# Mask rooms, mask loads and pinned copies in a single-core step of a hybrid decoder

## The chip, the cores and the metric

The kernel runs on one core of one Trainium2 chip. A core has a matrix engine (PE, with PEld for its weight loads), three elementwise engines (DVE, ACT, POOL) and SP, which only starts DMAs; ACT and POOL can start DMAs too. Each engine works through its own list of instructions in order and waits where an instruction needs something that another engine or a DMA hasn't finished. The metric is device time in microseconds (us) of one execution, and the median of some executions is compared. About 1%, some 9 us here, is what a measurement of this kernel can tell from no change.

## The reference, cut to what matters

One layer of a decoder for 1024 new prompt tokens and 8 single sampled tokens. All float32.

```python
proj = rms_norm(x, norm_g) @ w_in          # b, c, u, z (convolution), q, kv (3 branches), gates, z (attention)
q = rope(rms_norm(q, q_gain), pos) * HEAD_DIM ** -0.5
k = rope(rms_norm(kv[..., 0, :, :], k_gain), pos)
conv = b * (short_conv(c * u) + bias) * silu(z_conv)
kv_cmp = einsum('bcrjgd,rjde->bcjge', blocks_of_32(kv[cmp]) + cmp_pe, cmp_w)
# attention of a query block of 128: three branches, each with a mask of its own
for br in (cmp, slc, win):
    p = masked_softmax(q @ k_br.T, mask_br)
    o += sigmoid(gate[br]) * (p @ v_br)
y = x + concat([conv, o * silu(z_attn)]) @ w_out
sample_win_kv = concat([state_win_kv, new_row])[:, 1:]     # 8 state windows, moved by one row
```

## The kernel before, in words

Precision is kept by splitting each matrix operand in a high part (ACT's copy, `wh`, `hH`) and a low part (the difference, `wl`, `hL`, by DVE or POOL, line L80 for all of them), so each product is three matmuls.

**Stage 1** (`phase0`, 0 to 224 us) normalizes and transposes the tokens and projects them, tile by tile: first the rows of the compressed branch (`kv_tile` with branch 0), then those of the selected branch, then `gps`, the compression of 32-row blocks (64 matmuls of 66 columns, line L702), then the window branch, then the queries. Merged into it run the channel-wise products of one weight (`chan_mm`, lines L223 to L225, results in `mixA`). `norm_rope` (L262 to L273) is the chain of ACT and DVE operations that normalizes and rotates a tile's rows. `token_pairs` (L425) writes finished rows of the compressed branch into a tile `pr` by four DMAs, and `cmp_transposes` (L433) transposes `pr` on PE, so the PE's list holds a place at which it needs those DMAs. `cw_fetch` (L447) loads the compression weights in four chunks, each by four DMAs into the one room that has the tag `wx`, and each is split by ACT and DVE (tile `cw`) before `gps` can use it. `small_things` (L472 to L496) transposes a few small tables on PE: its `per2` is a copy by POOL (L476) into a room named `qn`, which `norm_rope` uses too.

**Attention** (`attn_stream`, 224 to about 660 us) goes over 32 units (a query block of 128, a group, a head pair). `prep` transposes the query (L903) and splits it (`q1`, `q2`); then scores (L931), softmax (DVE L919 with the mask tile, ACT L921), scaling (POOL L976, L980), transposes of P (L1005), their split, and the products with v (L1015). `masks` allocates the mask tile, clears part of it (POOL L881) and loads the rest by four DMAs (L883). Between the units stand the convolution's channel products (again L223 to L225, each followed by ACT L808 and DVE L809, which read the result out of its bank so that a later product may use it). `gate_rows` (16 small DMAs into `gr` and `grh`) and `window_copy` (8 copies of 511 KB from DRAM to DRAM, L864) are written among units 6 to 21; nothing reads them before the sample part late in the kernel.

The order on each engine isn't that of the code: a list scheduler places instructions by its own costs, and it may put one that is written late far ahead. `tc.keep_in_program_order`, which the change calls `keep`, holds an instruction behind all that was traced before it on its engine; it adds no wait. Rooms in SBUF are given by pools, and a tile that takes a room over waits for the last user of it.

Of the kernel before, what the change touches and what calls it, by code (L numbers as in the profile page):

```python
# [10 lines left out]
F32 = mybir.dt.float32  # L11
# [3 lines left out]
OP = mybir.AluOpType  # L15
# [5 lines left out]
NT = 9  # L21
# [40 lines left out]
def hymba_step_kernel(ctx, tc, io):  # L62
    nc = tc.nc
    WARM = 8
    PE, ACT, DVE, POOL, SP = nc.tensor, nc.scalar, nc.vector, nc.gpsimd, nc.sync
    SB, PSUM = bass.MemoryType.SB, bass.MemoryType.PSUM

# [3 lines left out]
    def f(ap):  # L71
        return ap.bitcast(F32)
# [38 lines left out]
    gr = cst.tile([64, 3], F32, name="gr")  # L111
    grh = cst.tile([32, 2, 3], F32, name="grh")
# [26 lines left out]
    for c in range(3):  # L139
        n = min(CH, NTOK - c * CH)  # L140
# [93 lines left out]
    rope0 = g2 = None  # L234

    def rope_tables(gain, slot, scale):

        SP.dma_start(g2[:, 0], bcast_rows(gain, 64))
        h0 = bass.AP(tensor=gain.tensor, offset=gain.offset + 32, ap=[[0, 128], [1, 32]])
        SP.dma_start(g2[:, 1, 0:32], h0)  # L240
        SP.dma_start(g2[:, 1, 32:64], bcast_rows(gain, 32))
        if scale != 1.0:
            DVE.tensor_scalar(g2, g2, scale, None, op0=OP.mult)
        v = mCf[:, 1152 + 1152 * slot:2304 + 1152 * slot].rearrange("p (i t d) -> p i t d", i=2, t=NT)
        for i in range(2):
            POOL.tensor_tensor(v[:, i], rope0[:, i], g2[:, i][:, None, :].to_broadcast([128, NT, 64]), OP.mult)
        return v[:, 0], v[:, 1]

    E0 = (ACT, POOL)
# [98 lines left out]
    wp = ExitStack()  # L348
    wk = wp.enter_context(pool("w0", "right"))
    rope0 = mCf[:, 0:1152].rearrange("p (i t d) -> p i t d", i=2, t=NT)  # L350
    hS = wk.tile([128, 8, 40], F32R, name="hS")
    POOL.memset(f(hS), 0.0)
    g2 = wk.tile([128, 2, 64], F32, name="g2", bufs=2)
    junk = mCf[:, 3456:3968].bitcast(mybir.dt.bfloat16)
    ROWS, ENDS = 2, 14000
    wl0 = w_loader(wk, 280, 2, 2, 1, 9)
    g1 = mCf[0:1, 2304:3328]
    one = mCf[0:1, 3968:4096]
# [8 lines left out]
    xsp = xss.enter_context(pool("xs"))  # L367
# [104 lines left out]
    def small_things():  # L472

        cvr, per, pti, spread = (small_in[n] for n in ("cvr", "per", "pti", "spread"))
        per2 = wk.tile([128, 512], F32, name="qn")[:32, :256].rearrange("p (j r d) -> p j r d", j=2, r=2)
        POOL.tensor_copy(per2, per.rearrange("p (j d) -> p j d", j=2)[:, :, None, :].to_broadcast([32, 2, 2, 64]))  # L476
        ptf = wk.tile([8, 16], F32, name="ptf")
        copy(DVE, ptf, pti)
        p = bank("tp")
# [11 lines left out]
        for r in range(2):  # L491
            q = slice(r * 64, r * 64 + 64)
            v = pv[q, :, :, r][:, :, None, :].to_broadcast([64, 2, 2, 16])
# [361 lines left out]
    def gate_rows(b):  # L855

        g = gates[b:b + 1, 8, :].rearrange("o (r t) -> o r t", t=3)
        SP.dma_start(gr[b * 8:(b + 1) * 8], g)
        SP.dma_start(grh[b % 4 * 8:b % 4 * 8 + 8, b // 4], g)

    def window_copy(b):

        src, dst = state_win[b], s_win[b]
        SP.dma_start(bass.AP(tensor=dst.tensor, offset=dst.offset, ap=[[8176, 16], [1, 8176]]),  # L864
                     bass.AP(tensor=src.tensor, offset=src.offset + 256, ap=[[8176, 16], [1, 8176]]))

    mask = P0 = wmask = None

    def masks():
        nonlocal mask, P0, wmask  # L870

        for v in (gates[:, 0:8], gates[:8, 8]):
            ACT.activation(v, v, AF.Tanh, scale=0.5)
            DVE.tensor_scalar(v, v, 1.0, 0.25, op0=OP.add, op1=OP.mult)
        POOL.memset(cu[:, 0:2], 0.0)


        mask = at.tile([128, 1212], F32, name="mask")
        P0 = at.tile([128, 2, 128], F32, name="P0")
        wmask = bass.AP(tensor=mask.tensor, offset=mask.offset, ap=[mask.ap[0], [832, 2], [1, 320]])  # L880
        POOL.memset(mask[:, 128:1024], 0.0)  # L881
        for dst, src, n in ((0, 0, 128), (1024, 512, 128), (1152, 864, 32), (1184, 644, 28)):
            SP.dma_start(mask[:, dst:dst + n], io["c_mask"][:, src:src + n])  # L883
        POOL.memset(P0, 0.0)


# [2 lines left out]
    def attn_stream():  # L889
        units = [(qi, g, hp) for qi in range(8) for g in range(2) for hp in range(2)]  # L890

        def double(u):
            qi, g, hp = u
            c = qi % 2 * 256 + hp * 128
            qd = at.tile([128, 2, 2, 64], F32, name="qd")
            v = qp[qi // 2][g][:, c:c + 128].rearrange("p (i d) -> p i d", i=2)
            POOL.tensor_copy(qd, v[:, :, None, :].to_broadcast([128, 2, 2, 64]))
            return qd

        def prep(qd):  # L900
            p = bank("pt")
            for i in range(2):
                PE.transpose(p[:, i * 128:i * 128 + 128], qd[:, i].rearrange("p r d -> p (r d)"), ident)  # L903
            q1 = at.tile([128, 2, 128], F32R, name="q1", bufs=2)
            q2 = at.tile([128, 2, 128], F32R, name="q2", bufs=2)
            pv = p[:, :256].rearrange("p (i c) -> p i c", i=2)
            copy(ACT, q1, pv)
            sub(DVE, q2, pv, f(q1))
            return q1, q2
# [111 lines left out]
        def finish(u, o):  # L1021
# [9 lines left out]
            if g == 1 and hp == 1:  # L1031
                done[qi] = True

        qq = prep(double(units[0]))
        masks()
        pend = []
        for ui, u in enumerate(units):
            o = [None]
# [715 lines left out]
```

## Time and profile before

| | |
|---|---|
| median of three runs | 928.27 us (921.03, 928.27, 930.33) |
| profiled execution | 926.67 us, its span 924.8 us |
| PE busy | 873.1 us (94%) |
| mean granted clock of PE | 0.983 |
| DVE, ACT, POOL busy | 577.0, 533.7, 402.3 us |
| DMA bytes | 91.12 MB, 99 GB/s over the span |

PE is the engine that the kernel waits for nearly all the time. A busy PE can still be slow: the profile gives the granted clock in shares of the higher of two levels (1.00 is 2.4 GHz, 0.50 is 1.2 GHz), and at 0.50 the same matmuls take twice as long while the busy share stays full. So lost time is read in two places, idle time of PE and stretches with a clock under 1.00.

### The profile page before, as it was taken

The numbers are of one execution on the slowest core, as the hardware profiler recorded it, in microseconds if no ns is written. First come the engines' busy times: TensorE is split into PE (matmuls) and PEld (weight loads), VectorE is DVE, ScalarE is ACT, GpSimd is POOL, SyncE is SP. The second block draws the span as 40 slices with busy tenths as digits, with TensorE's granted clock in tenths as the row PEclk, the third lists the DMA queues.
The fourth block names the chain that finished last, engine by engine and source line by source line (L and its number), as shares of the span: only waits on it lengthen the run. The fifth ranks groups of instructions, "written<-read, shape, count | busy, mean of one in ns | idle before, by whom it ended". The sixth has DMA issues, their size and how long they took to land.

```text
span 924.8 us, 16581 instructions
## 1 busy us (share of the span) xinstructions
PE 873.1 (94%) x5769; PEld 781.2 (84%) x5769; DVE 577.0 (62%) x1482; ACT 533.7 (58%) x1350; POOL 402.3 (44%) x547
## 2 busy tenths in 40 slices
PE   8889899999899999999989999999989999999987
PEld 6889899998689898899979898999877788677765
DVE  5866636687455555865775667667746555765663
ACT  5543325444466565665565755665756766687761
POOL 4332311112345444454344444444655444677751
PEclk9999979999889999999999999999999999999999
DMA  7433331651101000100010000000878552667621
GB/s 260 124 88 91 94 115 58 210 178 44 34 8 40 23 24 24 24 23 9 16 35 24 24 6 19 24 1 1 256 258 285 205 196 92 236 211 245 220 68 47
DMA packets 67154, 91.12 MB, mean 99 GB/s; under 512 B 19192, under 2 KB 49344, under 8 KB 64895
## 3 DMA queue, kind: packets, MB, share of 16 engines
q1 hardware_dynamic: 59004, 52.32, 18.7%
q0 software_dynamic: 8064, 37.75, 12.3%
q8 instruction: 45, 0.74, 0.4%
q14 instruction: 39, 0.31, 0.1%
q10 hardware_dynamic: 2, 0.00, 0.0%
HBM read 77.92 MB, written 15.29 MB: 101 GB/s over the span
## 4 chain that ended last, share of the span: by engine, by line
PE 47%; ACT 7%; DVE 7%; POOL 3%; issue 3%; DMA 2%; SPq 0%; ACTq 0%; DVEq 0%; POOLq 0%
PE o L1015 7%; PE pt L1005 5%; PE s L931 5%; PE mm L225 5%; PE mm L224 5%; PE mm L223 5%; POOL P L980 2%; PE om L1160 2%; PE mm L1572 1%; PE mm L1573 1%; PE mm L1574 1%; PE o L1456 1%; ACT P L921 1%; PE pt L1139 1%; PE s L1328 1%
## 5 line engine op out<-in xcount | busy, mean ns | idle before, releaser
L223 PE MATMUL mm<-hH,wh 128*128 128x384 f32 (+1 forms) x480 | 157.9, 329 | 3.7 <-DVE mixC L809 2.1
L225 PE MATMUL mm<-hH,wl 128*128 128x384 f32 (+1 forms) x480 | 155.0, 323 | 0.4 <-POOL wl L80 0.2
L224 PE MATMUL mm<-hL,wh 128*128 128x384 f32 (+1 forms) x480 | 154.8, 322 | 0.0
L80 POOL TENSOR_TENSOR wl<-wraw,wh 128x256 fp32r<-128x256 f32 (+1 forms) x105 | 77.6, 755 | 156.4 <-ACT wh L76 143.6
L921 ACT ACTIVATE P<-P,stat 128x640 f32<-128x640 f32 (+7 forms) x192 | 113.1, 591 | 36.8 <-DVE stat L919 36.1
L80 DVE TENSOR_TENSOR pl<-pt,ph 128x512 fp32r<-128x512 f32 (+1 forms) x164 | 102.7, 635 | 50.2 <-ACT ph L76 48.9
L76 ACT ACTIVATE ph<-pt 128x512 fp32r<-128x512 f32 (+1 forms) x164 | 88.4, 548 | 71.9 <-PE pt L1005 70.7
L980 POOL TENSOR_SCALAR P<-P,stat,gates 128x640 f32<-128x640 f32 (+7 forms) x128 | 99.9, 789 | 57.7 <-DVE stat L971 46.1
L1005 PE MATMUL pt<-ident,P 128*128 128x128 f32 x592 | 96.9, 281 | 6.2 <-POOL P L980 3.3
L931 PE MATMUL s<-k,q 128*128 128x320 f32 (+8 forms) x416 | 97.5, 337 | 2.5 <-DVE q L80 1.5
L223 PEld LDWEIGHTS mm<-hH,wh 128*128 128x128 f32 x480 | 91.1, 190 | 5.5 <-DVE mixC L809 3.3
L210 PE MATMUL mm<-wh,hL 128*128 128x256 f32 (+1 forms) x320 | 92.8, 291 | 1.6 <-DVE hL L80 1.6
L208 PE MATMUL mm<-wh,hH 128*128 128x256 f32 (+1 forms) x320 | 93.9, 294 | 0.1
L209 PE MATMUL mm<-wl,hH 128*128 128x256 f32 (+1 forms) x320 | 92.7, 290 | 0.9 <-POOL wl L80 0.9
L225 PEld LDWEIGHTS mm<-hH,wl 128*128 128x128 f32 x480 | 91.3, 190 | 1.1 <-POOL wl L80 1.0
L224 PEld LDWEIGHTS mm<-hL,wh 128*128 128x128 f32 x480 | 91.4, 190 | 0.2
L919 DVE CUSTOM_DVE_ANT_0 P<-s,mask 128x32 f32<-128x32 f32 (+8 forms) x160 | 70.9, 472 | 29.5 <-PE s L931 25.1
L1005 PEld LDWEIGHTS pt<-ident,P 128*128 128x128 f32 x592 | 71.0, 141 | 20.6 <-POOL P L980 10.6
L1015 PE MATMUL o<-ph,v 128*128 128x256 f32 x264 | 75.0, 303 | 1.7 <-ACT ph L76 1.1
L1015 PE MATMUL o<-pl,v 128*128 128x256 f32 x264 | 74.3, 303 | 1.6 <-DVE pl L80 1.5
L931 PEld LDWEIGHTS s<-k,q 128*128 128x128 f32 x416 | 67.9, 193 | 6.7 <-DVE q L80 1.7
L210 PEld LDWEIGHTS mm<-wh,hL 128*128 128x128 f32 x320 | 62.4, 195 | 2.0 <-DVE hL L80 2.0
(385 smaller groups left out, 2058.1 us busy)
## 6 DMA issues: line engine op xcount, KB each, us to landing
wraw<-in_w_in_dram SPq DMA_DIRECT2D x54, 256.0 KB
wo<-wo_d POOLq DMA_DIRECT2D x8, 512.0 KB, 4.6
out_s_win_dram<-in_state_win_kv_dram SPq DMA_DIRECT2D x8, 511.0 KB
xr<-in_x_prompt_dram SPq DMA_DIRECT2D x14, 256.0 KB
out_y_prompt_dram<-xr SPq DMA_DIRECT2D x14, 256.0 KB
sd<-in_state_win_kv_dram SPq DMA_DIRECT2D x5, 512.0 KB
mixA<-in_x_prompt_dram SPq DMA_DIRECT2D x4, 512.0 KB
xt<-in_x_prompt_dram SPq DMA_DIRECT2D x4, 512.0 KB
```

The costliest lines, as they stand in the source:

```text
L80: return eng.tensor_tensor(out, a, b, OP.subtract)
L208: PE.matmul(o[:, :n], hH[t // 3][:, k, s], wh, start=k == 0, stop=False)
L209: PE.matmul(o[:, :n], hH[t // 3][:, k, s], wl, start=False, stop=False)
L210: PE.matmul(o[:, :n], hL[t // 3][:, k, s], wh, start=False, stop=k == 7)
L223: PE.matmul(o[:, :n], wh, hH[c][:, k], start=k == 0, stop=False)
L224: PE.matmul(o[:, :n], wh, hL[c][:, k], start=False, stop=False)
L225: PE.matmul(o[:, :n], wl, hH[c][:, k], start=False, stop=k == 7)
L921: return lambda: ACT.activation(P, P, AF.Exp, bias=stt[:, 0, c:c + 1], scale=-1.0, accum_out=stt[:, 1, c:c + 1])
L931: PE.matmul(s[:, a:b], q[:, i], k, start=first, stop=not first)
L980: POOL.tensor_scalar(P[:, i, :n], P[:, i, :n], stt[:, 2, c + i:c + i + 1], gates[:, qi, gt:gt + 1], op0=OP.mult, op1=OP.mult)
L1005: PE.transpose(p[:, y * 256 + i * 128:y * 256 + i * 128 + 128], src[:, i], ident)
L1015: PE.matmul(o[0][:, :256], v, X[:, y * 256:y * 256 + 256], start=br == 1 and x == 0 and y == 0 and X is h[0], stop=last and y + 1 == len(p ...
```

## The change

It does five things. The rooms `rows` and `wx` are allocated ahead of all others of their pool, which moves the addresses: attention's mask tile now lies over `rows` and no longer over rooms that the last query's `norm_rope` uses. The four mask loads are issued by ACT, and `masks` is written ahead of the first `prep`, with the gates' sigmoids split out and left behind it. `per2` gets a tile of its own. `gate_rows` and `window_copy` are pinned on SP, and the two operations that build q's rotation table are pinned on POOL.

```diff
--- before.py
+++ after.py
@@ -62,6 +62,8 @@
 def hymba_step_kernel(ctx, tc, io):
     nc = tc.nc
     WARM = 8
+
+    keep = tc.keep_in_program_order
     PE, ACT, DVE, POOL, SP = nc.tensor, nc.scalar, nc.vector, nc.gpsimd, nc.sync
     SB, PSUM = bass.MemoryType.SB, bass.MemoryType.PSUM
 
@@ -243,7 +245,9 @@
             DVE.tensor_scalar(g2, g2, scale, None, op0=OP.mult)
         v = mCf[:, 1152 + 1152 * slot:2304 + 1152 * slot].rearrange("p (i t d) -> p i t d", i=2, t=NT)
         for i in range(2):
-            POOL.tensor_tensor(v[:, i], rope0[:, i], g2[:, i][:, None, :].to_broadcast([128, NT, 64]), OP.mult)
+            r = POOL.tensor_tensor(v[:, i], rope0[:, i], g2[:, i][:, None, :].to_broadcast([128, NT, 64]), OP.mult)
+            if scale != 1.0:
+                keep(r)
         return v[:, 0], v[:, 1]
 
     E0 = (ACT, POOL)
@@ -348,11 +352,14 @@
     wp = ExitStack()
     wk = wp.enter_context(pool("w0", "right"))
     rope0 = mCf[:, 0:1152].rearrange("p (i t d) -> p i t d", i=2, t=NT)
+    ROWS, ENDS = 2, 14000
+
+    wk.tile([128, 512], F32, name="rows", bufs=ROWS)
+    wk.tile([128, 2, 280], F32, name="wx")
     hS = wk.tile([128, 8, 40], F32R, name="hS")
     POOL.memset(f(hS), 0.0)
-    g2 = wk.tile([128, 2, 64], F32, name="g2", bufs=2)
+    g2 = wk.tile([128, 2, 64], F32, name="g2")
     junk = mCf[:, 3456:3968].bitcast(mybir.dt.bfloat16)
-    ROWS, ENDS = 2, 14000
     wl0 = w_loader(wk, 280, 2, 2, 1, 9)
     g1 = mCf[0:1, 2304:3328]
     one = mCf[0:1, 3968:4096]
@@ -472,7 +479,7 @@
     def small_things():
 
         cvr, per, pti, spread = (small_in[n] for n in ("cvr", "per", "pti", "spread"))
-        per2 = wk.tile([128, 512], F32, name="qn")[:32, :256].rearrange("p (j r d) -> p j r d", j=2, r=2)
+        per2 = xsp.tile([32, 256], F32, name="per2").rearrange("p (j r d) -> p j r d", j=2, r=2)
         POOL.tensor_copy(per2, per.rearrange("p (j d) -> p j d", j=2)[:, :, None, :].to_broadcast([32, 2, 2, 64]))
         ptf = wk.tile([8, 16], F32, name="ptf")
         copy(DVE, ptf, pti)
@@ -855,24 +862,26 @@
     def gate_rows(b):
 
         g = gates[b:b + 1, 8, :].rearrange("o (r t) -> o r t", t=3)
-        SP.dma_start(gr[b * 8:(b + 1) * 8], g)
-        SP.dma_start(grh[b % 4 * 8:b % 4 * 8 + 8, b // 4], g)
+        keep(SP.dma_start(gr[b * 8:(b + 1) * 8], g))
+        keep(SP.dma_start(grh[b % 4 * 8:b % 4 * 8 + 8, b // 4], g))
 
     def window_copy(b):
 
         src, dst = state_win[b], s_win[b]
-        SP.dma_start(bass.AP(tensor=dst.tensor, offset=dst.offset, ap=[[8176, 16], [1, 8176]]),
-                     bass.AP(tensor=src.tensor, offset=src.offset + 256, ap=[[8176, 16], [1, 8176]]))
+        keep(SP.dma_start(bass.AP(tensor=dst.tensor, offset=dst.offset, ap=[[8176, 16], [1, 8176]]),
+                          bass.AP(tensor=src.tensor, offset=src.offset + 256, ap=[[8176, 16], [1, 8176]])))
 
     mask = P0 = wmask = None
 
-    def masks():
-        nonlocal mask, P0, wmask
+    def sigmoids():
 
         for v in (gates[:, 0:8], gates[:8, 8]):
             ACT.activation(v, v, AF.Tanh, scale=0.5)
             DVE.tensor_scalar(v, v, 1.0, 0.25, op0=OP.add, op1=OP.mult)
         POOL.memset(cu[:, 0:2], 0.0)
+
+    def masks():
+        nonlocal mask, P0, wmask
 
 
         mask = at.tile([128, 1212], F32, name="mask")
@@ -880,7 +889,7 @@
         wmask = bass.AP(tensor=mask.tensor, offset=mask.offset, ap=[mask.ap[0], [832, 2], [1, 320]])
         POOL.memset(mask[:, 128:1024], 0.0)
         for dst, src, n in ((0, 0, 128), (1024, 512, 128), (1152, 864, 32), (1184, 644, 28)):
-            SP.dma_start(mask[:, dst:dst + n], io["c_mask"][:, src:src + n])
+            ACT.dma_start(mask[:, dst:dst + n], io["c_mask"][:, src:src + n])
         POOL.memset(P0, 0.0)
 
 
@@ -1031,8 +1040,9 @@
             if g == 1 and hp == 1:
                 done[qi] = True
 
+        masks()
         qq = prep(double(units[0]))
-        masks()
+        sigmoids()
         pend = []
         for ui, u in enumerate(units):
             o = [None]
```

What it moves: first PE, in stage 1. Tile `tp_850` (`tp_852` after) is the bank of `small_things`, `mm_905` the last product of the compressed branch, `mm_970` a channel product. Before:

```order
L212 MATMUL mm_905<-wh_206,hS_120 40x256
L484 MATMUL tp_850<-ident_58,qn_846 128x32 x2
L213 MATMUL mm_905<-wl_207,hS_120 40x256
L212 MATMUL mm_905<-wh_210,hS_120 40x256
L213 MATMUL mm_905<-wl_211,hS_120 40x256
L223 MATMUL mm_970<-hH0_96,wh_635 128x384
```

After, the two transposes of `per2` stand with the other small ones:

```order
L440 MATMUL tp_820<-ident_58,pr1_224 128x128 x4
L488 MATMUL tp_852<-ident_58,cvr_221 128x20 x4
L489 MATMUL tp_852<-ident_58,ptf_850 16x8
L491 MATMUL tp_852<-ident_58,per2_848 128x32 x2
L226 MATMUL mm_873<-hL2_101,wh_236 128x264
```

And seven matmuls into `mm_1010`, the first tile of the selected branch, PE now needs the last `pr` tile (`pr1_224`):

```order
L211 MATMUL mm_1010<-wl_480,hH0_96 128x256
L212 MATMUL mm_1010<-wh_479,hL0_97 128x256
L210 MATMUL mm_1010<-wh_545,hH0_96 128x256
L440 MATMUL tp_933<-ident_58,pr1_224 128x128 x4
L507 MATMUL tp_940<-ptT_860,spread_222 128x8
L510 MATMUL tp_940<-ptT_860,spread_222 128x4 x2
L211 MATMUL mm_1010<-wl_546,hH0_96 128x256
```

Before, the same four transposes stood 57 matmuls further on, in the next tile's product: the wait on `qn` is gone from the list, and the need for `pr` is earlier.

Second DVE, ahead of `gps`: the split of the fourth chunk of compression weights (`cw`). Before it stood behind the sample rows of the selected branch:

```order
L266 TENSOR_TENSOR qn<-srows_90,rs 8x128
L267 TENSOR_TENSOR srows_90<-qn,mixC 8x128
L271 TENSOR_TENSOR rb<-qn,mixC 8x2x32 x2
L273 TENSOR_TENSOR srows_90<-srows_90,rb 8x128
L80 TENSOR_TENSOR cw<-cwr,cw 128x8x64
L80 TENSOR_TENSOR wl<-wx,wh 128x280
```

After, it stands inside the rows of the third pair of tiles:

```order
L270 TENSOR_TENSOR qn<-rows,rs 128x256
L271 TENSOR_TENSOR rows<-qn,mixC 128x256
L275 TENSOR_TENSOR rb<-qn,mixC 128x4x32 x2
L82 TENSOR_TENSOR cw<-cwr,cw 128x8x64
L277 TENSOR_TENSOR rows<-rows,rb 128x256
L82 TENSOR_TENSOR k_1004<-tp,k_1004 64x2x256
L79 COPY kd_1279<-rows 128x512
L82 TENSOR_TENSOR wl<-wraw,wh 128x280 x2
```

It moved ahead of all the sample rows and the weight splits, and on PE the 64 matmuls of `gps` now stand in one piece, where before 20 matmuls of the window branch stood between the first 24 and the other 40.

Third DVE, where attention begins. `mm_2986`, `mm_3075` and `mm_3167` are the three parts of a channel product (128, 128 and 8 columns of tokens); L919 is the masked part of the softmax. Before:

```order
L80 TENSOR_TENSOR q2_2954<-pt_2950,q1_2953 128x256
L809 SCALAR_TENSOR_TENSOR mixC_75<-mixC_75,mm_2986 128x384
L809 SCALAR_TENSOR_TENSOR mixA_76<-acc_3207,mixA_76 128x4x128
L80 TENSOR_TENSOR q2_3038<-pt_3034,q1_3037 128x256
L809 SCALAR_TENSOR_TENSOR mixA_76<-acc_3315,mixA_76 128x4x8
L809 SCALAR_TENSOR_TENSOR mixA_76<-acc_3696,mixA_76 128x4x128
L809 SCALAR_TENSOR_TENSOR mixA_76<-acc_4302,mixA_76 128x4x128
L809 SCALAR_TENSOR_TENSOR mixC_75<-mixC_75,mm_3075 128x384
L809 SCALAR_TENSOR_TENSOR mixC_75<-mixC_75,mm_3167 128x264
L919 ISA P1_2970,stat_2972<-s_2975,mask_2962 128x128
L919 ISA stat_2972 128x1
```

After:

```order
L82 TENSOR_TENSOR q2_2964<-pt_2960,q1_2963 128x256
L928 ISA P1_2972,stat_2974<-s_2977,mask_2950 128x128
L928 ISA stat_2974 128x1
L928 ISA P1_2972,stat_2974<-s_3015,mask_2950 128x128
L928 ISA stat_2974 128x1
L928 ISA P0_2951,stat_2974<-s_2977,mask_2950 128x32
L928 ISA stat_2974 128x1
L928 ISA P0_2951,stat_2974<-s_3015,mask_2950 128x32
L928 ISA stat_2974 128x1
L816 SCALAR_TENSOR_TENSOR mixA_76<-acc_3028,mixA_76 128x4x128
L928 ISA P2_2973,stat_2974<-s_3031,mask_2950 128x128
L928 ISA stat_2974 128x1
```

The softmax of the first unit now stands right behind its query's split, ahead of the read-out of the channel products, which before came first. On PE the second and third part of that product, before in one piece, are now cut by the first units' transposes and products.

## Rows read from the trace of the kernel before

**Rows 1.** What PE waited for, 0 to 240 us: total us, times, longest.

```profile
PE tp L484 <- POOL qn L476: 2.7, 1, 2.7
...
PE gps L702 <- DVE cw L80: 2.6, 1, 2.6
```

**Rows 2.** Stretches: length, busy us of PE, PEld, DVE, ACT, POOL, PEclk, DMA, GB/s.

```profile
60.00:72.00 12.00, 9.33 (x68) 8.97 (x67) 6.67 (x19) 5.15 (x15) 8.61 (x12) 1.00 0.24 60
116.00:128.00 12.00, 12.00 (x62) 11.90 (x61) 3.29 (x9) 3.59 (x13) 2.61 (x3) 0.57 0.70 218
228.00:262.00 34.00, 28.50 (x134) 23.43 (x132) 17.26 (x71) 16.96 (x60) 12.87 (x28) 0.80 0.13 35
```

**Rows 3.** Shorter stretches of the beginning of attention, same columns.

```profile
234.00:236.00 2.00, 2.00 (x7) 2.00 (x7) 1.30 (x2) 0.63 (x1) 0.00 (x0) 0.50 0.00 0
...
250.00:252.00 2.00, 2.00 (x11) 2.00 (x11) 1.21 (x9) 1.07 (x5) 0.00 (x0) 0.50 0.51 127
```

**Rows 4.** Timelines where attention begins: start, length, engine, line, operation, count, [idle <- releaser].

```profile
231.72 0.45 PE L931 MATMUL s<-k,q 128*128 128x160 f32 x2 [1.46 <-DVE q L80]
...
259.38 1.52 PE L1005 MATMUL pt<-ident,P 128*128 128x128 f32 x4
...
231.26 0.41 DVE L80 TENSOR_TENSOR q<-pt,q 128x256 fp32r<-128x256 f32 x1
...
243.34 0.28 DVE L919 CUSTOM_DVE_ANT_0 P<-s,mask 128x128 f32<-128x128 f32 x1
...
225.74 1.28 ACT L808 ACT_TABLE_LOAD   x1
...
228.06 1.77 SPq L883 DMA_DIRECT2D mask<-in_c_mask_dram  x4
```

**Rows 5.** Timeline of PE around the two transposes of `per2`.

```profile
63.47 0.28 PE L212 MATMUL mm<-wh,hS 128*40 128x256 f32 x1
66.42 0.31 PE L484 MATMUL tp<-ident,qn 32*128 32x32 f32 x2 [2.67 <-POOL qn L476]
...
67.04 0.34 PE L223 MATMUL mm<-hH,wh 128*128 128x384 f32 x1
...
71.21 0.28 PE L208 MATMUL mm<-wh,hH 128*128 128x256 f32 x1
```

**Rows 6.** Timelines of POOL and of DVE around the copy and `norm_rope`.

```profile
60.51 4.47 POOL L80 TENSOR_TENSOR wl<-wraw,wh 128x256 fp32r<-128x256 f32 x6 [15.00 <-ACT wh L76]
65.73 0.64 POOL L476 COPY qn<-mixC 32x256 f32<-32x256 f32 x1 [0.75 <-DVE rb L271]
...
62.02 0.70 DVE L196 SCALAR_TENSOR_TENSOR rs<-rs 128x4 f32<-128x4 f32 x1
...
65.69 0.43 DVE L273 TENSOR_TENSOR rows<-rows,rb 128x256 f32<-128x256 f32 x1
...
67.30 0.22 DVE L80 TENSOR_TENSOR XL<-tp,XH 64x64 fp32r<-64x64 f32 x1
...
84.50 0.16 DVE L196 SCALAR_TENSOR_TENSOR rs<-rs 128x4 f32<-128x4 f32 x1
```

**Rows 7.** Timelines of SP's DMA issues and of ACT's split behind one of them.

```profile
66.28 2.97 SPq L425 DMA_DIRECT2D pr<-rows  x4
...
90.00 2.67 SPq L447 DMA_DIRECT2D cwr<-in_cmp_w_dram  x4
...
94.93 0.64 ACT L76 ACTIVATE cw<-cwr 128x512 fp32r<-128x512 f32 x1 [0.69 <-DMA cwr<-in_cmp_w_dram]
```

**Rows 8.** Timelines of DVE and of POOL ahead of the second part of `gps`.

```profile
113.91 0.67 DVE L80 TENSOR_TENSOR cw<-cwr,cw 128x512 fp32r<-128x512 f32 x1
...
112.39 3.48 POOL L246 TENSOR_TENSOR mixC<-mixC,g 128x576 f32<-128x576 f32 x2 [3.63 <-DVE srows L267]
```

**Rows 9.** All matmuls of `gps` that read `XH`: length min/median/max in ns, first and last start.

```profile
L702 PE MATMUL gps<-XH,cw x32: 220/285/402, 106.6 to 120.9; 128*128 128x66 f32 x32
```

**Rows 10.** What ACT waited for before its weight splits, 262 to 520 us.

```profile
ACT wh L76 <- PE mm L224: 2.1, 8, 0.3
```

## The prediction

> **What bounds the kernel now.** PE is busy 94% of the span, so I read first where it is idle and where its clock is low, and only then what the others do. The list of PE's waits up to 240 us [rows 1] has two long ones in stage 1: 2.7 us for POOL's copy into `qn` (L484) and 2.6 us for the last split of the compression weights ahead of `gps` (L702). Both are single events, at 63.8 and 112.0 us. The stretches [rows 2] tell what followed. Around the first the clock stays at 1.00. After the second, from 116 to 128 us, PE is busy all 12 us, at a mean granted clock of 0.57: it had fallen to the lower level, 1.2 GHz, some 2 us after PE resumed. At full clock the same work would take 12 x 0.57 = 6.8 us, so that stretch loses 5.2 us. I take 4.6 of them, because its first and last two microseconds are mixed. The third loss is where attention begins: from 228 to 262 us PE is idle 34.0 - 28.5 = 5.5 us and the mean clock is 0.80, which costs another 34 x 0.20 = 6.8 us; 12.3 us in all [rows 2]. The clock is at 0.50 there twice, around 234 to 236 and for five stretches alike from 250 to 260 us [rows 3]. Before the first fall PE had waited 1.5 us for a query's split [rows 4]. From there on to 520 us PE's time is work; no edit can shorten that.
>
> **The change part by part.** The terms are set against the profiled execution, 926.67 us. It lies 1.6 us below the median of the three runs, and I add that at the end.
>
> *per2, and the need for pr (about 0.3 us lost).* Before, PE stands from 63.59 (the last start, 63.47, and 0.12 for one matmul) to 66.42, a gap of 2.83 us [rows 5]. POOL's copy had to wait until `norm_rope` was through with the room `qn`, for 0.75 us behind the six splits, and took 0.64 [rows 6]. With a room of its own the copy is done long before, and this gap goes. What is late next is `pr`. In PE's list the four transposes of the last `pr` tile now stand right behind: 3 more matmuls and 2 transposes of `per2` (0.6 us), 4 transposes of the other `pr` tile (0.6), the channel product's 24 (67.04 to 71.21, 4.2 us [rows 5]), and 7 of `mm_1010` (0.8). 63.6 + 6.2 = 69.8 us is when PE asks for them. The DMAs that fill that tile were issued from 66.28 on, 2.97 us for the four, right behind the rotation's last operation (65.69 + 0.43 [rows 6, 7]). Loads of the same shape took 94.93 - 92.67 = 2.3 us from the end of their issue to the first use [rows 7]. If the rotation were done as early as before, `pr` would be there at 66.28 + 2.97 + 2.3 = 71.5 us, already 1.7 us too late. I expect it later. While POOL runs its weight splits, DVE operations with two inputs in SBUF take their turn with it: the same 4-column operation lasted 0.70 us at 62.02 and 0.16 at 84.50, and one that reads PSUM was not held up (0.22 at 67.30) [rows 6]. Before, POOL's pause of 0.75 us at 65.0 let the last three rotation operations through; after, all eleven of its splits (six of them in 4.47 us, 0.745 each) run without one, to 60.51 + 11 x 0.745 = 68.7 us. Three operations at 0.75 in place of some 0.37 each end 1.2 us later, so issue from 67.5, landing at 72.8: PE waits 3.0 to 3.1 us where it waited 2.83. Bounds: -1.1 (the rotation at its old time) to +1.5 (the seven small operations of `small_things`, which now stand in the same chain, come on top of it in full, some 1.2 us).
>
> The Trainium skill, on the page "SBUF — State Buffer", section "Who interferes with whom", says that DVE and GpSimd hold a shared pair of ports as an exclusive lock for a whole instruction, and that a DVE operation contends if both its inputs are in SBUF. The pairs of durations above agree with it; if every operation of the chain had to wait out a whole POOL split it would be the upper bound, +1.5.
>
> *The last cw split and gps (2.6 us and 4.6 us won).* The four chunks are loaded one after the other, each when the split of the chunk before has freed the room. Before, the fourth split came only at 113.91 us, behind the sample rows, one of which was held up by POOL's rotation table at 112.39 [rows 8]. After, I step the chain: chunk 2 can be issued at about 77 us, behind the `pr` wait; each further chunk costs 2.67 us of issue, 2.3 of landing, and about 1.3 for ACT's and DVE's part [rows 7], when the chain isn't held by rows; with the rows between them I get 83.7, 90 and 96.4 us for the splits. PE came to `gps` at 106.6 [rows 9]. So there are 10 us to spare, and the wait of 2.6 us [rows 1] goes. The rotation table, pinned behind later work, is no longer there either, and its next user is the first query, tens of microseconds later. With the idle time gone I let the fall of the clock behind it go too: 4.6 us. Bounds: 0 to -2.6 for the wait, 0 to -5.2 for the clock.
>
> *Where attention begins (5.5 us won).* The mask tile lay over a room of the last query's `norm_rope`, its loads were issued by SP only at 228.06 us [rows 4], and the first masked softmax came at 243.34, 12 us after the split that gives it its query (231.26 [rows 4]). After, the loads' only waits are on stores of the output weights, which land near 200 us. ACT issues them at about 225.7, 4 x 0.44 us by SP's row, before its table load of 1.28 us, which is pushed back by as much; the masks are there well before 231 us. The first softmax then starts at about 231.2. What takes over: PE's second part of the channel product needs the read-out of the first (DVE L809), and that now stands behind six softmaxes and a convolution step. These six take 0.2 to 0.3 us each and the step 0.7 to 0.9, so the read-out ends at 233.0 to 233.6, and PE begins that part 1.4 us later than before (231.72 + 0.45 = 232.2 [rows 4]). In return, the units' transposes and products run between the parts from 235.9 us on. Stepped with full clock, the four transposes that before began at 259.38 and let the next matmul start at 260.7 [rows 4] are done at 252.5: 8.2 us earlier, so 12.3 - 8.2 = 4.1 us of idle time stay. The clock I don't expect to be full: PE still has little to do between 229.5 and 237 us. I put 1.7 us for a fall like that of 234 to 236 us and 1.0 for a part of the second: 8.2 - 2.7 = 5.5. Bounds: -8.2 (no fall) to -1.4 (6.8 us lost to the clock as before).
>
> By the Trainium skill ("DMA: Bandwidth & Descriptors", section "Issuing engines are not separate DMA queues") a move of DMAs from one engine to another saves only the issuing engine's time, since all run on the same 16 DMA engines. By that rule ACT's queue in itself is worth nothing here; the row agrees so far as SP's issue took 1.77 us and PE waited on none of it. What I count comes from the rooms and from the order, not from the queue.
>
> *The pinned copies (0).* Eight copies of 511 KB and 16 small DMAs leave SP in stage 1 (0.5 to 0.7 us of issue each) and come among the weight loads of attention. There ACT waits for PE before its weight splits, 2.1 us in all, and never for a load [rows 10]: the loads are early, and this cover hides the copies. If it is gone, see the last rival.
>
> The sum: 0.3 - 2.6 - 4.6 - 5.5 = -12.4, so 914.3 us by the profiled execution, and 915.9 with the 1.6 us to the median. The four terms' bounds as they are give 908 to 926 with the less likely ends cut.
>
> **The rivals.**
>
> *The clock falls elsewhere.* The new wait at 69.8 us is a little longer than both of stage 1 before, of which one was followed by a fall and the other wasn't. A fall there, or within the 64 matmuls of 66 columns that now stand in one piece, costs what the row shows, 4.6 to 5.2 us: 920.5 to 921. For it: waits of 2.6 and 1.5 us were followed by falls. Against it: the wait of 2.67 us wasn't.
>
> *Attention's beginning gives nothing back.* The softmax comes earlier, but the channel product waits for its bank and the clock stays low over the same stretch; only 1.4 us are won: 920.0. For it: the read-out was moved behind the softmaxes. With the clock's fall in stage 1 as well, 925.
>
> *The change does not do what it says.* Something else holds the mask or the `cw` chain, so that both big waits stay and only the copies move: 926 to 929.
>
> *Slower.* The weight loads of attention come late. SP works in order; 24 DMAs stand ahead of weight loads at some 13 places among units 6 to 21, and a copy that waits for a free slot holds up the load behind it. If each place makes ACT's split, and so PE, late by x, the kernel loses 13x. It ends slower than before by 1% from 13x = 12.4 + 9.3, x = 1.7 us at every place; at 2 us it gives 942. Against it: that these loads were never waited for [rows 10].
>
> **How the numbers follow.** Forecast 0.43 (own range 911 to 919), clock falls elsewhere 0.25, attention gives nothing 0.14, both of these 0.06, the change does nothing 0.06, slower 0.06. Faster by over 1% means below 919.0: nearly all of the forecast's case, and a third of the next two: 0.55. Slower by over 1% is 0.06, and the rest, 0.39, within 1%, which is about what a measurement of this kernel can tell from no change. The range, 908 to 926 us, takes in all but the ends of the bounds, the slower case, and a part of the case in which nothing happens.
>
> **What would show it.** No wait at L491 and a wait of about 3 us at L440 near 70 us; none at L709 (`gps`) and a clock of 1.00 from 112 to 128 us, shifted; the fourth `cw` split near 96 us; the first masked softmax within 1 us of its query's split; from 228 to 262 us less than 7 us lost, idle and clock together; no wait of ACT on a weight load in 300 to 500 us. I am wrong if the clock falls in a place where it was full, or if attention's first units, cut into pieces by the channel product, leave PE as sparse as it was.

## The result, and the profile after

The changed kernel takes 922.0 us, the median of eight runs (919.1 to 925.9), beside 927.95 us before: a ratio of 0.9937, 95% interval 0.9911 to 0.9962. The forecast was 915.9 us, in a range of 908 to 926. About half of the expected gain came (6.0 of 12.4 us). The profiled execution took 922.36 us, 4.3 less than the one of before.

The list of PE's waits after, up to 240 us, first line, answers to [rows 1]: both entries are gone, and the wait for `pr` has come in. Lines of the changed kernel have numbers 2 to 9 higher than before (L440 was L433, L709 was L702).

```profile
PE tp L440 <- DVE rb L275: 2.3, 1, 2.3
```

Stretches of the changed kernel, columns as in [rows 2] (length, busy us of PE, PEld, DVE, ACT, POOL, PEclk, DMA share, GB/s):

```profile
72.00:76.00 4.00, 4.00 (x19) 3.65 (x18) 2.27 (x6) 1.12 (x2) 1.88 (x2) 0.50 0.30 84
...
108.00:112.00 4.00, 4.00 (x39) 4.00 (x37) 3.90 (x7) 2.01 (x7) 3.54 (x5) 1.00 0.47 134
112.00:120.00 8.00, 8.00 (x40) 8.00 (x40) 4.89 (x22) 1.75 (x7) 0.00 (x0) 0.52 0.36 99
...
192.00:200.00 8.00, 6.14 (x28) 5.74 (x29) 6.67 (x15) 1.69 (x5) 1.10 (x1) 0.64 0.09 33
228.00:262.00 34.00, 29.35 (x165) 25.09 (x163) 19.43 (x83) 19.02 (x66) 15.67 (x33) 0.90 0.14 36
```

Behind the `pr` wait the clock is at 0.50, which it wasn't in the same place before. At 112 us it falls again, though PE had been busy without a gap: no wait stands ahead of `gps` any more. In 192 to 200 us there are idle time and a low clock that the kernel before doesn't have: it was busy for all 8.00 us there at 1.00, as this row of it shows:

```profile
192.00:200.00 8.00, 8.00 (x69) 8.00 (x68) 7.09 (x18) 2.92 (x7) 0.74 (x1) 1.00 0.56 174
```

From 228 to 262 us the loss is 34.00 - 29.35 = 4.65 us idle and 34 x 0.10 = 3.4 by the clock, 8.1 in place of 12.3 [rows 2].

Timelines of the changed kernel: SP's loads and PE's transposes of `pr`, DVE's split of the fourth `cw` chunk, the first two and the last two of the 64 `gps` matmuls, PE at the queries' weights, ACT's split of these, DVE's first masked softmax, and the four transposes of the third unit.

```profile
67.18 2.60 SPq L432 DMA_DIRECT2D pr<-rows  x4
71.35 1.09 PE L440 MATMUL tp<-ident,pr 128*128 128x128 f32 x4 [2.33 <-DVE rb L275]
97.32 0.69 DVE L82 TENSOR_TENSOR cw<-cwr,cw 128x512 fp32r<-128x512 f32 x1 [0.63 <-ACT cw L78]
107.91 0.22 PE L709 MATMUL gps<-XH,cw 128*128 128x66 f32 x1
107.95 0.27 PE L709 MATMUL gps<-XL,cw 128*128 128x66 f32 x1
...
117.03 0.40 PE L709 MATMUL gps<-XH,cw 128*128 128x66 f32 x1
117.24 0.40 PE L709 MATMUL gps<-XL,cw 128*128 128x66 f32 x1
...
192.12 0.39 PE L210 MATMUL mm<-wh,hH 128*128 128x256 f32 x1 [0.51 <-ACT wh L78]
193.31 0.39 PE L211 MATMUL mm<-wl,hH 128*128 128x256 f32 x1 [0.80 <-POOL wl L82]
194.86 0.58 PE L211 MATMUL mm<-wl,hH 128*128 128x256 f32 x1 [0.94 <-DVE wl L82]
...
191.66 0.72 ACT L78 ACTIVATE wh<-wraw 128x256 fp32r<-128x256 f32 x2 [1.10 <-DMA wraw<-in_w_in_dram]
...
232.04 0.42 DVE L82 TENSOR_TENSOR q<-pt,q 128x256 fp32r<-128x256 f32 x1
232.89 0.29 DVE L928 CUSTOM_DVE_ANT_0 P<-s,mask 128x128 f32<-128x128 f32 x1 [0.43 <-PE s L940]
...
255.22 1.43 PE L1014 MATMUL pt<-ident,P 128*128 128x128 f32 x4
```

To see where the 4.3 us lie, the same instruction is sought in both traces:

| instruction | before | after | after - before |
|---|---|---|---|
| PE, selected branch, behind `pr` | 80.54 | 82.53 | +2.0 |
| PE, window branch, behind `gps` | 126.62 | 125.21 | -1.4 |
| DVE, last rotation of the last query | 229.35 | 230.89 | +1.5 |
| PE, third unit's four transposes | 259.38 | 255.22 | -4.2 |
| PE, output product (`om`) | 697.10 | 693.83 | -3.3 |
| whole execution | 926.67 | 922.36 | -4.3 |

So stage 1 loses 1.5 us in all, the beginning of attention gains 5.7, and what differs after it is back at the end. (The clock falls there in both executions, but not in the same places: for 3.4 us near 472 us before, for 6.8 us near 679 us after.)

### The profile page after: what moved, and what is told of

Read it like the earlier page. It is cut to its first block, busy times and chain, and to the rows that moved or that the text cites. A ratio compares the mean times of both kernels' runs of the same rounds, so it can differ in the third digit from the quotient of the medians.

```text
span 920.6 us, 16583 instructions
## 1 busy us (share of the span) xinstructions
PE 874.4 (95%) x5769; PEld 784.8 (85%) x5769; DVE 576.8 (63%) x1482; ACT 532.7 (58%) x1350; POOL 400.5 (44%) x547
## 3 DMA queue, kind: packets, MB, share of 16 engines
q0 software_dynamic: 8064, 37.75, 12.3%
## 4 chain that ended last, share of the span: by engine, by line
PE 47%; ACT 7%; DVE 7%; issue 3%; POOL 3%; DMA 2%; SPq 0%; ACTq 0%; DVEq 0%; POOLq 0%
PE o L1024 7%; PE pt L1014 5%; PE s L940 5%; PE mm L227 5%; PE mm L225 5%; PE mm L226 5%; POOL P L989 2%; PE om L1170 2%; ACT P L930 1%; PE mm L1582 1%; PE mm L1583 1%; PE o L1466 1%; PE mm L1584 1%; PE pt L1149 1%; ACT ph L78 1%
## 5 line engine op out<-in xcount | busy, mean ns | idle before, releaser
L211 PE MATMUL mm<-wl,hH 128*128 128x256 f32 (+1 forms) x320 | 95.2, 297 | 1.7 <-DVE wl L82 0.9
L212 PE MATMUL mm<-wh,hL 128*128 128x256 f32 (+1 forms) x320 | 94.9, 296 | 1.2 <-DVE hL L82 1.2
L1014 PEld LDWEIGHTS pt<-ident,P 128*128 128x128 f32 x592 | 70.3, 140 | 19.3 <-POOL P L989 10.2
L210 PEld LDWEIGHTS mm<-wh,hH 128*128 128x128 f32 x320 | 64.4, 201 | 2.4 <-ACT hH L78 1.4
```

The costliest lines, as they stand in the source:

```text
L210: PE.matmul(o[:, :n], hH[t // 3][:, k, s], wh, start=k == 0, stop=False)
L211: PE.matmul(o[:, :n], hH[t // 3][:, k, s], wl, start=False, stop=False)
L1014: PE.transpose(p[:, y * 256 + i * 128:y * 256 + i * 128 + 128], src[:, i], ident)
```

## The experiments

Ratios are to the kernel before, run on the same chip (medians of before 926.7 us for e1 to e4, 927.5 for e5 to e8, 927.3 for e9 to e11).

| | median us | ratio, 95% interval |
|---|---|---|
| e1 gps at 264 columns | 924.0 | 0.9973 (0.9949 to 0.9997) |
| e2 change without the SP pins | 923.8 | 0.9970 (0.9953 to 0.9988) |
| e3 rooms and masks alone | 923.1 | 0.9955 (0.9933 to 0.9978) |
| e4 SP pins alone | 918.2 | 0.9909 (0.9876 to 0.9942) |
| e5 gps at 132 columns | 916.2 | 0.9874 (0.9842 to 0.9905) |
| e6 need for `pr` later | 917.4 | 0.9882 (0.9848 to 0.9916) |
| e7 change without the masks' move | 917.6 | 0.9900 (0.9862 to 0.9938) |
| e8 e5, e6 and e7 joined | 912.0 | 0.9831 (0.9797 to 0.9865) |
| e9 the change again | 921.0 | 0.9922 (0.9895 to 0.9950) |
| e10 e5 and e6 joined | 912.8 | 0.9837 (0.9798 to 0.9876) |
| e11 before, gps at 132 columns | 920.8 | 0.9929 (0.9904 to 0.9953) |

**e1.** Is it the wait or `gps` itself after which the clock falls?

```diff
-                    PE.matmul(o[:, :66], cw[:, rho, j], X[:, 2 * j:2 * j + 2, rho::16],
+                    PE.matmul(o[:, :264], cw[:, rho, j], X[:, 2 * j:2 * j + 2, rho::16][:, None].to_broadcast([128, 4, 2, 33]),
```

> The changed kernel, in which each of the 64 gps matmuls streams its 66 columns four times over (264 columns; the first 66 are read). Nothing else moves. In the changed kernel a gps matmul of 66 columns started every 0.111 us (107.95 to 110.51, 23 steps) and one of 264 columns every 0.12 us, so the added columns cost 64 x 0.01 = 0.6 us. Theory (it is gps's own narrow run, not a wait ahead of it, after which the clock fell at 112 us): clock 1.00 from 108 to 124 us, 5.1 us won, 0.6 lost: 922.0 - 4.5 = 917.5 us. Rival (the fall follows from something that went before, the wait at 70 us or the rows around it, or comes whatever gps streams): the fall stays, 10.24 us long, and 922.0 + 0.6 to 1.2 = 922.6 to 923.2 us.

The clock did what the theory says, the time didn't: 924.0 us, where 917.5 was expected. A stretch of e1:

```profile
112.00:128.00 16.00, 16.00 (x102) 15.12 (x102) 3.76 (x15) 3.56 (x14) 0.73 (x1) 1.00 0.07 21
```

And its timeline at the start of `gps`:

```profile
104.58 0.41 PE L709 MATMUL gps<-XL,cw 128*128 128x264 f32 x1
104.80 0.41 PE L709 MATMUL gps<-XH,cw 128*128 128x264 f32 x1
105.03 0.41 PE L709 MATMUL gps<-XL,cw 128*128 128x264 f32 x1
```

The clock is 1.00 throughout, but these matmuls start 0.226 us apart, not 0.12, so the columns cost 64 x (0.226 - 0.111) = 7.4 us, and 922.0 - 5.1 + 7.4 = 924.3. My price came from matmuls that read their columns side by side; these read one float in 16.

**e2.** The whole change, with the pins of SP taken out:

```diff
-        keep(SP.dma_start(gr[b * 8:(b + 1) * 8], g))
+        SP.dma_start(gr[b * 8:(b + 1) * 8], g)
```

(and the same for `grh` and `window_copy`).

> The whole change without the pins of gate_rows and window_copy on SP. Theory (the pins brought the need for pr forward on PE, and with it the wait of 2.33 us and the fall of the clock at 72 us, 3.4 us lost, and they brought the order of q's weights at 192 us with 2.25 us of waits and 3.4 us of clock): per2's wait of 2.7 us is gone, nothing replaces it, no fall at 72 and at 193 us, gps again in two pieces with a wait for the fourth cw split of up to 2.6 us and a fall behind it; attention as in the changed kernel, 5.7 won. 927.95 - 2.7 - 5.7 = 919.5 us. Rival (the places of the falls are not bound to this order; what is won at one place is lost at the next): 922 us, as the changed kernel. Second rival (without the pins the copies again share queues with stage 1's loads, and this was worth something): 923 or more.

The two places are as expected, the total (923.8 us) isn't. Stretches of e2, first around `gps`, then at the queries' weights:

```profile
112.00:128.00 16.00, 11.18 (x60) 10.26 (x59) 5.80 (x17) 3.35 (x12) 2.63 (x3) 0.63 0.40 123
184.00:192.00 8.00, 8.00 (x63) 8.00 (x62) 6.96 (x18) 5.01 (x12) 2.63 (x2) 1.00 0.70 224
192.00:200.00 8.00, 8.00 (x65) 8.00 (x64) 7.30 (x18) 3.73 (x10) 0.74 (x1) 1.00 0.60 207
```

Without the pins, there is neither wait nor fall at 192 us. But from 112 to 128 us PE is idle for 4.8 us (1.4 for the `cw` split, 2.4 for `kc`, 0.7 for a weight) and the clock is at 0.63: the 3 us that it was ahead of the kernel before at 64 us are gone by 129 us (129.29 before, 129.77 in e2). The first rival described this better than the theory. The second rival's 923 us fits the number as well, but that shared queues did it isn't shown: for `cw` and `kc` PE waited on DVE, not on a load.

**e3.** The kernel before with the hunks on the rooms, `masks` and the mask loads alone.

```diff
-            SP.dma_start(mask[:, dst:dst + n], io["c_mask"][:, src:src + n])
+            ACT.dma_start(mask[:, dst:dst + n], io["c_mask"][:, src:src + n])
...
+        masks()
         qq = prep(double(units[0]))
-        masks()
+        sigmoids()
```

> The kernel before with the rooms and the mask loads alone (rows and wx first, masks ahead of the first prep, loads by ACT); per2, the pins of SP and of POOL as before. Stage 1 keeps its order on PE. Theory (where attention begins is worth what the traces show, 5.7 us, and by itself): 927.95 - 5.7 = 922.2 us, both waits of stage 1 and the fall at 114 us as before. Rival (the gain there hangs on the other parts, or a fall of the clock takes it back): 926 to 928 us.

923.1 us, a gain of 3.6 us on this chip where 5.7 was expected; the interval (2.0 to 6.2 us) takes both in. In the trace, e3 is 5.3 us behind the kernel before at 225 us and 1.4 us behind at 260 (the channel products' matmuls that start at 225.01 and 260.66 before), so the beginning of attention gains 3.9. In this execution the clock was low behind the old wait at L484 (0.80 from 66 to 72 us), with the instruction order of before, where it had stayed at 1.00.

**e4.** The kernel before with the pins of e2's diff and nothing else.

> The kernel before with the pins of gate_rows and window_copy on SP alone. PE then needs pr early (as in the changed kernel) and has gps in one piece. Theory (the pins cost nothing in attention; in stage 1 they take gps's wait of 2.6 us away and give a wait and a fall of 3.4 us near 72 us; gps's own fall stays): 927.95 - 2.6 + 3.4 = 928.8 us, and up to 934 if the order of q's weights at 192 us also comes from them. Rival (the pins alone are a gain, since gps's wait goes and the clock is not bound to this): 925.3 us or less.

The theory fell: the pins alone are worth at least as much as the whole change (918.2 us; the intervals overlap). Stage 1 has little part in it: the 2.7 us wait for `qn` stays, PE then comes to `pr` without waiting, and at 225 us e4 is 0.2 us ahead of the kernel before. From there to 260 us it gains 7.4. In e4, SP's mask loads, the query's split on DVE and the first masked softmax:

```profile
227.21 1.76 SPq L885 DMA_DIRECT2D mask<-in_c_mask_dram  x4
...
230.48 0.41 DVE L82 TENSOR_TENSOR q<-pt,q 128x256 fp32r<-128x256 f32 x1
...
231.33 0.29 DVE L921 CUSTOM_DVE_ANT_0 P<-s,mask 128x128 f32<-128x128 f32 x1
```

The loads are in the old room, on the old queue and 0.85 us earlier than before (228.06 [rows 4]); the softmax is 12 us earlier. What was in its way before was its place in DVE's list, behind the read-outs of the channel product, and not the mask. The operation right ahead of it in the kernel before:

```profile
242.99 0.43 DVE L809 SCALAR_TENSOR_TENSOR mixC<-mixC,mm 128x264 f32<-128x264 f32 x1 [3.69 <-ACT mixC L808]
```

DVE stood idle for 3.69 us in front of that read-out, and the softmax followed at 243.34. In e4 the mask was in use 2.4 us after the end of its issue (228.97 us); before, its issue ended at 229.83, 13.5 us ahead of the softmax.

**e5.** e1 with 132 columns (`o[:, :132]`, `[128, 2, 2, 33]`).

> The changed kernel with each gps matmul streaming its 66 columns twice (132 columns, the first 66 read); e1 showed that 264 columns took 0.226 us each where 66 took 0.111, so four times was not free: 64 x 0.115 = 7.4 us. At 264 columns / 0.226 us, 132 columns would stream in 0.113 us, about the 0.111 us that each matmul takes anyway. Theory (the clock falls in gps because of gps's own narrow matmuls): at 132 columns gps takes 7.2 us and the clock either stays at 1.00 to 124 us (5.1 us won, 917 us) or falls later and shorter (1.7 to 3.4 us won, 918.6 to 920.3). Rival (what cleared the fall in e1 was the longer time or the missing fall at 72 us, not the columns): fall as before, 922 us.

916.2 us, by the theory. Stretches of e5, around the `pr` wait and over `gps` (104.21 to 111.6, one matmul each 0.116 us):

```profile
66.00:72.00 6.00, 3.66 (x27) 3.30 (x25) 4.49 (x13) 2.64 (x7) 4.12 (x6) 1.00 0.40 103
72.00:78.00 6.00, 6.00 (x52) 6.00 (x52) 2.43 (x5) 1.28 (x3) 1.21 (x1) 1.00 0.25 67
102.00:110.00 8.00, 8.00 (x71) 8.00 (x69) 7.74 (x16) 4.44 (x14) 5.73 (x8) 1.00 0.52 144
110.00:118.00 8.00, 8.00 (x66) 8.00 (x65) 3.25 (x17) 1.90 (x8) 0.00 (x0) 1.00 0.29 88
```

PE's list and the number of matmuls are those of the change. The columns alone took the fall away. The `pr` wait is still 2.3 us, and here nothing fell behind it. That the missing fall at 72 us was the cause, as the rival has it, is ruled out by e7 below, whose list on PE is that of the change up to 226 us. With 66 columns it has no fall at 72 us either, and the clock falls in `gps`:

```profile
72.00:78.00 6.00, 6.00 (x52) 5.98 (x52) 2.90 (x6) 1.32 (x3) 1.76 (x2) 1.00 0.23 59
108.00:116.00 8.00, 8.00 (x39) 8.00 (x39) 4.31 (x17) 1.05 (x4) 0.40 (x1) 0.51 0.36 99
```

Of all profiles with `gps` in one piece, the five with 66 columns (the change, e4, e6, e7, e9) have the clock at 0.50 there for 10.2 us, and the four with more columns (e1, e5, e8, e10) have it at 1.00.

**e6.** The changed kernel with the last transposes due later:

```diff
-                ... cmp_transposes(pr, t - 1), 4 if t < 5 else 3 if t < 7 else 1))
+                ... cmp_transposes(pr, t - 1), 4 if t < 5 else 3 if t < 7 else 5))
```

> The changed kernel with the last transposes of the compressed rows (the need for pr) due four steps later, which puts them 44 matmuls further on in PE's list, about 5 us; the two matmuls on the tables go a little earlier and nothing else on PE moves. Theory (per2's wait was not removed but moved to pr, and the clock falls behind it in most executions): wait of 2.33 us at L440 gone and no fall at 72 us: 922.0 - 2.3 - (0 to 3.4) = 916.3 to 919.7 us. Rival (the DVE chain is late by itself, so that the wait comes back at the next reader, the cw splits or the selected branch's rows): 921 to 923 us.

917.4 us, in the expected range. Stretch of e6:

```profile
60.00:72.00 12.00, 12.00 (x91) 11.77 (x90) 9.72 (x29) 6.67 (x19) 9.56 (x13) 1.00 0.43 117
72.00:78.00 6.00, 6.00 (x54) 6.00 (x53) 1.16 (x1) 2.22 (x5) 3.20 (x3) 1.00 0.25 61
```

No wait and no fall there; the fall in `gps` stays. A wait of 1.4 us for `kd` at 85 us takes some of it back.

**e7.** The changed kernel with the masks as they were before (e3's diff turned round; the pins, rooms and `per2` stay).

> The changed kernel without the move of the masks: they stay behind the first prep and on SP, with the sigmoids in one function; rooms, per2 and all pins as in the change. Theory (it is the pins that free SP for the masks: in e4, with the pins alone, SP issued them at 227.21 us and the first masked softmax began at 231.33, so where attention begins the mask's move adds nothing, and its order, with the read-out of the channel product behind six softmaxes, costs the 0.9 us wait and 3.4 us of clock more): 922.0 - 2 to 4 = 918 to 920 us, with first softmax near 232 and PE as in e4 (clock 0.96 in 224 to 262 us). Rival (e4 was better only because its stage 1 had no fall at 72 us): 922 us.

917.6 us, and the clock from 224 to 262 us is 1.00 (0.91 in the change). The interval (0.9862 to 0.9938) overlaps that of the change, so this alone doesn't settle what the masks' move costs; e10 takes it up.

**e8.** e5's, e6's and e7's edits in one kernel.

> e5, e6 and e7 in one: pins, rooms and per2 of the change, masks left on SP, the need for pr later, gps at 132 columns. If the parts add up: 922.0 - 2.3 - 1.7 (half of a fall at 72 us) - 3.4 to 5.1 (gps) - 2 to 4 (attention) = 908.9 to 912.6 us. Rival (what is cleared at one place falls at the next, as between before and the change): 916 us or more.

912.0 us, within the sum, and 1.1% under the changed kernel (0.9831 beside 0.9937, intervals apart). Stretches of e8 over the three places in stage 1:

```profile
60.00:72.00 12.00, 12.00 (x91) 11.77 (x90) 10.31 (x25) 5.84 (x17) 9.55 (x13) 1.00 0.50 133
...
100.00:120.00 20.00, 20.00 (x165) 19.73 (x164) 13.75 (x41) 9.48 (x32) 6.80 (x9) 1.00 0.36 95
180.00:192.00 12.00, 10.02 (x68) 9.41 (x67) 9.76 (x23) 3.87 (x9) 1.47 (x2) 0.86 0.20 67
```

What is left in stage 1 are the queries' weights.

**e9.** The changed kernel as it is.

> The changed kernel once more, for its ratio on a chip beside e10 and e11 and for a second profile. Theory (the fall at 72 us behind the 2.33 us wait is not in every execution: e1, e5 and e7 had the same wait without it): a profile with the wait at L440 and either a fall of 6.83 us behind it or none, 3.4 us apart; the fall in gps near 112 us and the waits near 192 us are there again. Median 0.9937 of before within 0.3%. Rival (the fall belongs to the order of this kernel alone): again a fall of 6.83 us at 72 us.

The ratio is that of the first measurement. The fall behind the `pr` wait was there again (0.50 from 72 to 76 us). With the same wait of 2.3 us, behind the same list on PE, two profiles show it (the change, e9) and three don't (e1, e5, e7). The 2.7 us wait for `qn` is alike: the clock stays at 1.00 around it before and in e4, and falls in e3 and e11. The runs of e9 go from 914.98 us at a mean clock of 0.991 to 923.80 at 0.979, so the falls differ from one execution to the next. What decides it stays open.

**e10.** e8 with the masks' move of the change, that is, e5's and e6's edits in the changed kernel.

> e8 with the move of the masks as in the change (e5 and e6 in one). Theory (with the pins, the move of the masks costs where attention begins: e7 was 2 to 4 us faster without it): 911.96 + 2 to 4 = 914 to 916 us, with the 0.9 us wait for the read-out of the channel product (DVE mixC) and a fall of 6.83 us near 227 us. Rival (e7's lead came from the missing fall at 72 us, and the masks' move is worth nothing either way): 911 to 913 us.

912.8 us: the rival. The 0.9 us wait for `mixC` and the lower clock (0.91 from 220 to 256 us) are in the profile, but the ratios are 0.06% apart. Beside the pins the masks' move neither helps nor hurts by what the times can tell. The place itself speaks against it: between the two matmuls named under e3, the eight profiles with the move gain 3.9 to 5.7 us, each with 6.8 us at the low clock; the four with an early softmax but without the move (e4, e7, e8, e11) gain 6.3 to 7.6, with 3.4 us at the low clock or none.

**e11.** The kernel before with e5's edit alone.

> The kernel before with gps at 132 columns and no other edit; its 64 matmuls then also stand in one piece, ahead of 20 matmuls of the next branch, so the wait for the fourth cw split stays and grows, to 2.6 to 7 us. Theory (the columns of gps decide, not the wait): the clock is 1.00 behind the wait, through gps and up to 128 us. Rival (the step of the prediction: the clock falls behind the wait): it falls within some 4 us of PE's return and stays low for 10 us. Time 927.95 - 5.1 + 0 to 2 = 923 to 925 us by the theory, 928 to 931 by the rival; later stages are ordered a little differently, so the clock of 108 to 128 us decides, not the total.

Here the rival was right on the clock. The timeline of e11 at the end of the wait ahead of the last 40 `gps` matmuls:

```profile
114.72 0.48 PE L702 MATMUL gps<-XH,cw 128*128 128x132 f32 x1 [5.09 <-DVE cw L80]
```

And the stretches around it:

```profile
112.00:114.00 2.00, 0.00 (x0) 0.00 (x0) 1.93 (x6) 0.00 (x0) 1.53 (x2) 0.64 0.17 53
114.00:122.00 8.00, 7.28 (x34) 7.28 (x35) 2.48 (x4) 1.73 (x5) 4.57 (x4) 0.50 0.70 203
```

PE is idle for 5.09 us and the clock falls before it is back: with 132 columns, too, a wait of this length is enough. The total (920.8 us) is better than either theory because the edit also reordered the beginning of attention. SP issued the masks at 230.00 us, later than before, into the old room, and the first masked softmax came at 235.10, 1.9 us behind its query's split. One matmul of the channel products starts at 225.01 before and at 227.53 in e11, a later one at 260.66 and 256.27: e11 wins 6.9 us in between, with none of the change's parts.

## Why the prediction was wrong

**The step that failed** is the one behind `gps`: "With the idle time gone I let the fall of the clock behind it go too: 4.6 us." The wait of 2.6 us did go, and the `cw` chain came as stepped (splits at 83.9, 90.2 and 97.3 us where 83.7, 90 and 96.4 were forecast). It went with SP's pins and not with POOL's: e4 has only SP's and no such wait, e2 has only POOL's and waits 1.4 us. The fall stayed: 10.2 us at 0.50 in both profiled executions, 5.1 us lost in each. e5 shows why: with the same list and no wait, 64 matmuls of 66 columns are followed by the fall, and the same 64 with 132 columns aren't. The "clock falls elsewhere" rival had named this case, "within the 64 matmuls of 66 columns", as a chance. Its 920.5 to 921 us lie near the measured 922.0 partly by luck: it counted one fall, and there were two, and the loss at the queries' weights besides. e11 keeps the other half of the step alive: a wait of 5.1 us brings the clock down with 132 columns too. Which of the two did it in the kernel before isn't shown. There the fall began at 116.7 us, 2.1 us after a wait of 2.6 and among the narrow matmuls, and a wait of 2.6 us ahead of wide ones was not run. Without the wait, the narrow matmuls were enough.

**The need for `pr`** was right as a wait: one of 2.33 us in place of 2.67, where 3.0 to 3.1 was forecast. Issue began at 67.18 us (67.5 forecast), and the loads needed 1.6 us from the end of issue to the first use instead of 2.3 (which was taken from loads out of DRAM; these go from SBUF to SBUF). What the sum lacked is the fall behind it, 3.4 us in the profiled execution. e6 shows the size of both together: its ratio is 0.40 to 0.55% under the two of the change, 3.7 to 5.1 us, though its interval overlaps both.

**The queries' weights**, 2.9 us net between `gps` and the last query, stand in no term. Their last load is issued at about the same time in both kernels (188.43 before, 188.91 after), and ACT's split follows at about 191.6 in both. Before, PE still had a channel product to do from 187.9 to 192 us. After, that product runs from 185.1 to 189.5 us, and PE comes to the weights before they are split: 0.51, 0.80 and 0.94 us of waiting, then a low clock. e2 and e3, without the pins, don't have this; e4 and e7, with them, do. The prediction put the pins at nothing, and in attention that holds: the changed kernel is 4.2 us ahead at 260 us and 4.3 at the end, and ACT waits for no weight load in 300 to 500 us. Their price is in stage 1, through the order.

**Where attention begins** came out at 5.7 us where 5.5 was forecast, but only in part for the reason given. The prediction counted the rooms and the order, and took the mask's room and its late loads for what held the softmax. e4 and e11 load it into the old room through SP, e11 even later than before, and the softmax is early in both. It is DVE's list that held it back, and an edit that reorders that list can win these microseconds: the masks' move (e3), the pins (e4) or something unrelated (e11). The gains don't add: e10 beside e8 shows no difference. The sign "less than 7 us lost" from 228 to 262 us was missed, at 8.1. As to the queue, the Trainium skill ("DMA: Bandwidth & Descriptors", section "Issuing engines are not separate DMA queues") gives the move to ACT no value of its own; e4 and e11 agree, with SP issuing the loads and the softmax 0.9 and 1.9 us behind the query's split.

The sum with the measured terms, in the profiled execution: +2.7 around `pr` (its fall 3.4, less the shorter wait), -3.4 from there to behind `gps` (the wait of 2.6, one of 0.4 for `kd`, and small things; nothing for the clock, where 4.6 was forecast), +2.9 at the queries' weights, -5.7 in attention. From the -0.7 at which the two traces stand ahead of `pr`, that is -4.2; the whole is -4.3. The slower rival didn't come. The prediction's range has a slip of its own: the bounds of its four terms add up to 911 to 928 us by the median, not 908 to 926.

## What to carry to other kernels

Where a low clock follows a wait, look at what PE runs in that stretch before you credit the clock to the wait: narrow matmuls back to back can be the cause by themselves, and repeating their columns up to the time that each one takes anyway is a cheap test and, here, a gain (0.5 to 0.6%, e5 beside the two runs of the change). When a late operation has its data long before it starts, read the engine's list: the order may hold it, and then any edit that reorders may win the time, but only once. An edit that only pins an order should be costed at every place where the order changes, also where nothing of it runs.

## What the runs showed of the hardware

A `gps` matmul takes 0.111 us with 66 columns, 0.116 with 132 and 0.226 with 264, while one of 264 columns that lie side by side takes 0.12. So `gps`, which reads one float in 16, streams at about half the rate, and this doesn't show until the columns take longer than the rest of the matmul. That the step of 16 is the cause is argued, since e1 also reads the same columns four times. The Trainium skill ("SBUF — State Buffer", section "Door 1: The DMA port swizzle") says that SBUF needs more than one access to a 16-byte line for full bandwidth; it gives no factor, and the 1.9 here agrees with it in direction.

The granted clock can fall while PE's busy share is full: from 108 to 112 us of the changed kernel PE is busy 4.00 of 4.00 us, in narrow matmuls, and the clock then drops to 0.50; with 132 columns in the same list it stays at 1.00 (e5). And the same wait of 2.3 us, in the same list, is followed by a fall in one execution (e9) and not in another (e1, e5).
